# Fused two-block kernel: an opening stage with a hand-written matmul order, grouped modulation sums, and the gate half of convolution group 1 in the two tap banks

## The chip, the cores and the metric

The kernel runs on one core of a Trainium2 chip. Its engines are TensorE (PE; PEld is its weight load), VectorE (DVE), ScalarE (ACT) and GpSimd (POOL); SyncE (SP) issues the DMAs. The metric is the device time of one execution in microseconds (us): the median of three runs.

## The reference, cut to what matters

Two blocks on a sequence of 512 tokens and width 1024, batch 1, all in float32: a first block with two layers (mLSTM and convolution mixer, then an MLP), and a second block (convolution and neighbourhood attention). The change touches the start of layer 0 of the first block:

```python
mod = c_act @ w_ada[l] + b_ada[l]          # c_act = silu(c); 1024 -> 6 x 1024
sh_mix, sc_mix, gt_mix, sh_mlp, sc_mlp, gt_mlp = split(mod, 6)
h = rms_norm(x, g_pre_mix[l]) * (1 + sc_mix) + sh_mix
u = h @ w_in[l]                            # 1024 -> 4096
x_m, z, glu_a, glu_b = split(u, 4)
...
a = glu_a * sigmoid(glu_b)
a = causal_depthwise_conv(a, w_dw, b_dw)   # 31 taps per channel
a = silu(group_layer_norm(a, 8, g_cn, b_cn))
return concat([h_m, a], -1) @ w_out[l]
```

## The kernel before, in words

Activations lie feature-major: 8 tiles `hT[f]` of 128 features by 512 tokens. Every float32 product is made of three matmuls on a high and a low part: `mm3` (L164 to L166) multiplies `wh` with `h` high, `wh` with `h` low, and `wl` with `h` high. A weight unit is loaded by SP into one of 3 buffers `wr`, cast by ACT to `wh` (L155, L1314), and the rest `wl = wr - wh` is made by DVE or POOL (`sub`, L143); `wh` and `wl` have 4 buffers each.

PSUM has three pools: 4 banks `mm` for products, 2 banks `tr` for transposes and small sums, 2 banks `cv` for the long convolution.

**Opening.** `proj_start` makes columns 2048 to 2303 (the value half of convolution group 0) and 3072 to 3327 (its gate half) of layer 0's `w_in` in 4 `mm` banks, in 4 steps `p` of 2 features tiles each: 24 matmuls a step. Before a step, `stage(p)` must have made its two `hT` tiles: `ada_first` adds up 256 shift and 256 scale columns of `w_ada` in 8 matmuls of 32 columns (L439; four of them share the array at four column positions) as each 256 KB load lands, ACT copies the sums (L444), PE transposes them (L447), DVE finishes `mf` (L449, L450, L391); PE transposes the normalised `xn` (L218), ACT scales and shifts it (`hx`, L224), and DVE writes the high and low halves of `h` (L231, L143). For `p == 0`, `x` is loaded and normalised too (L195 to L205).

**Convolution.** There are 4 groups of 256 channels. `glu_cons(g)` makes the gated input `glu` of a group on ACT (L601) and DVE (L602). `taps(g)` puts the group's last tap with the bias into the two `cv` banks on ACT (L584), adds 30 taps to each bank on DVE (L589, 60 instructions a group) and copies both banks to `cacc` on ACT (L593). The `cv` banks serve one group at a time, so group g+1 begins when ACT has copied group g out. `conv_norm` (transposes L696, copies L697, statistics L700 and L701, scaling L711), `conv_gate` (L719, L721, L723, L724) and `conv_split` (L730, `cg`) follow for each group, and the out projection reads `cg`. Between the convolution groups PE makes the rest of `w_in` (`xproj(h)`, with `xm_cons` on ACT and DVE: L628 to L643; `qkv(h)`, whose results ACT copies at L662 and whose transposed `v` it copies at L675; `zproj`).

**What sets the order.** SP issues in program order (`manual_schedule` on SP). On PE, DVE, ACT and POOL a scheduler sets the order when the program is built, by priority, and each engine then runs its queue strictly in that order. `taps` has a much lower priority than all else (`with low(LOWP)`), its ACT instructions as well.

Of the kernel before, what the change touches and what calls it, by code (L numbers as in the profile page):

```python
# [46 lines left out]
def fused_blocks_kernel(ctx: ExitStack, tc: tile.TileContext, I, out):  # L47
# [210 lines left out]
    def proj_start(stage, hT, consumer):  # L258

        ps = [mm() for _ in range(4)]  # L260
        cur = stage(0)
        for p in range(4):
            if p < 3:
                nxt = stage(p + 1)
            h, lo = cur
            for i in range(4):
                for k in range(2):
                    kt, w = 2 * p + k, 2 * (i // 2) + k
                    c = slice((i % 2) * 128, (i % 2) * 128 + 128)
# [158 lines left out]
    def ada_first(p):  # L428


        ps = long_bank()
        wv = wada[0][:, :, 0:2048].rearrange("p k (g n) -> p k g n", g=2)[:, :, :, p * 256:p * 256 + 256]
        for kt in range(0, 8, 2):
            raw = A([128, 2, 2, 256], F32, "wr")
            for k in range(2):
                SP.dma_start(raw[:, k], wv[:, kt + k])
            for k in range(2):
                g = (kt + k) % 4
                PE.matmul(ps[32 * g:32 * g + 32, :], crep[:, kt + k], raw[:, k].rearrange("p g n -> p (g n)"),  # L439
                          start=kt < 4, stop=kt >= 4, tile_position=(0, 32 * g))  # L440
            free(raw)
            yield
# [129 lines left out]
    def mixer(l, pre, units, nxt, pre_next):  # L572
# [34 lines left out]
        if l == 0:  # L607
            proj_start(units, hT, glu_cons(0))
        else:
            proj_first(units, hT, lambda: pre.turn(1), glu_cons(0))  # L610
        for g in range(1, 4):
            projA(wi, [2048 + 256 * g, 3072 + 256 * g], hT, glu_cons(g), eng=None if l == 0 and g == 2 else P)
        free(glu[0])

        if l == 0:
            load_const()
            free(crep)
        q, k, vf, v1, tz, xmh, xch = {}, {}, {}, {}, {}, {}, {}
        wg = A([128, 4, 6, 32], F32, "wg")
        SP.dma_start(wg, I["wg"][l])  # L620

        def xm_cons(h):
# [22 lines left out]
            return fn  # L645

# [648 lines left out]
    def stage(p):  # L1295

        lead = ada_first(p)
        if p == 0:
            for t in range(2):
                next(lead)  # L1300
                load_x(t)
                mix[0].post(t)
        for _ in lead:
            pass
        if p == 0:
            for t in range(2, 4):
                load_x(t)
                mix[0].post(t)
        raw = wrp.tile([128, 4, 256], F32, tag="wr", name="wr")
        for i, c0 in enumerate((2048, 3072)):  # L1310
            SP.dma_start(raw[:, 2 * i:2 * i + 2], wi_[0][:, 2 * p:2 * p + 2, c0:c0 + 256])
        h = whp.tile([128, 4, 256], F32R, tag="wh", name="wh")
        lo = wlp.tile([128, 4, 256], F32R, tag="wl", name="wl")
        S.copy(h, raw)  # L1314
        sub(lo, raw, h, P)
# [116 lines left out]
```

## Time and profile before

| | before |
|---|---|
| median of 3 runs | 2286.89 us (2286.07 to 2290.43) |
| profiled execution, its own time | 2287.21 us |
| its span, first to last instruction | 2285.2 us |
| mean granted TensorE clock | 0.994 |
| PE busy | 2240.0 us (98%) |
| DVE busy | 1530.7 us (67%) |
| ACT busy | 979.1 us (43%) |
| POOL busy | 301.3 us (13%) |

The profile is of one execution. Times in rows are us from the start of the span. A row of the timeline has the start, the length, the engine, the line, the operation, `out<-in` by the program's names, the count, and in brackets the idle time before it with the engine and line that ended it. Ends of matmuls are modelled, so lengths of neighbours overlap; the distance between two starts is the pace. A 32-column sum in float32 shows as two records.

### The profile page before, as it was taken

To read this page: it belongs to the slowest core of one execution; us is meant where nothing else is said; L and a number is where in the kernel's file an instruction comes from. 1 tells how busy PE (TensorE), PEld (TensorE's weight loads), DVE (VectorE), ACT (ScalarE), POOL (GpSimd) and SP (SyncE) were. 2 spreads that over 40 slices of the span, in tenths; PEclk is the share of its full clock that TensorE was granted. 3 is DMA by queue.
4 is the path that set the end of the run, shared out by engine and by line. 5 is a ranking of instruction groups with operands and counts; after the bars stand their busy time and mean duration, and the time that the engine had idled before them with its cause. 6 is when DMAs were issued, how large, how long until landed. Compare 5 with 4: busy or idle time off the path is not lost.

```text
span 2285.2 us, 29859 instructions
## 1 busy us (share of the span) xinstructions
PE 2240.0 (98%) x11164; PEld 1807.5 (79%) x11164; DVE 1530.7 (67%) x3037; ACT 979.1 (43%) x1651; POOL 301.3 (13%) x263
## 2 busy tenths in 40 slices
PE   8999999999999999999999999999999999999998
PEld 3777677878777888767887778888888888878886
DVE  4898998874555678899887643387566574652345
ACT  3557554543323334666543332235545554222232
POOL 1763000000000144400000000000321311000000
PEclk9999999999999999999999999999999999999999
DMA  7632134366565232321436544523211321532331
GB/s 265 211 116 79 55 120 131 128 198 194 179 190 176 87 117 85 92 65 47 148 120 187 177 127 127 170 75 114 88 50 54 98 77 60 172 95 94 99 131 65
DMA packets 194585, 277.69 MB, mean 122 GB/s; under 512 B 13812, under 2 KB 146548, under 8 KB 194440
## 3 DMA queue, kind: packets, MB, share of 16 engines
q1 hardware_dynamic: 194440, 275.78, 37.8%
q8 instruction: 88, 1.44, 0.3%
q14 instruction: 57, 0.47, 0.1%
HBM read 263.68 MB, written 14.37 MB: 122 GB/s over the span
## 4 chain that ended last, share of the span: by engine, by line
PE 74%; DVE 5%; ACT 2%; issue 1%; DMA 0%; POOL 0%; SPq 0%; DVEq 0%; ACTq 0%; POOLq 0%
PE mm L166 22%; PE mm L165 22%; PE mm L164 22%; PE cv L1129 1%; PE tr L1114 1%; PE mm L827 1%; PE mm L851 1%; PE mm L1093 0%; PE mm L1095 0%; DVE h L143 0%; PE tr L218 0%; DVE nt L176 0%; ACT sb L1103 0%; DVE h L231 0%; ACT junk L195 0%
## 5 line engine op out<-in xcount | busy, mean ns | idle before, releaser
L164 PE MATMUL mm<-h,wh 128*128 128x512 f32 (+1 forms) x1728 | 656.8, 381 | 3.8 <-DVE h L231 2.9
L165 PE MATMUL mm<-h,wh 128*128 128x512 f32 (+1 forms) x1728 | 654.3, 379 | 0.7 <-DVE h L143 0.6
L166 PE MATMUL mm<-h,wl 128*128 128x512 f32 (+1 forms) x1728 | 654.4, 379 | 0.1
L155 ACT CAST wh<-wr 128x1024 fp32r<-128x1024 f32 (+1 forms) x318 | 323.3, 1018 | 532.4 <-PE mm L165 249.7
L143 DVE TENSOR_TENSOR wl<-wr,wh 128x1024 fp32r<-128x1024 f32 x254 | 314.0, 1240 | 224.4 <-ACT wh L155 223.4
L164 PEld LDWEIGHTS mm<-h,wh 128*128 128x128 f32 x1728 | 324.7, 188 | 75.2 <-DVE h L231 6.8
L166 PEld LDWEIGHTS mm<-h,wl 128*128 128x128 f32 x1728 | 324.8, 188 | 68.3 <-issue 5.9
L165 PEld LDWEIGHTS mm<-h,wh 128*128 128x128 f32 x1728 | 325.3, 188 | 66.1 <-issue 3.0
L589 DVE SCALAR_TENSOR_TENSOR cv<-glu,vec,cv 128x511 f32<-128x511 f32 (+24 forms) x480 | 327.8, 732 | 7.1 <-ACT cv L584 6.8
L362 DVE SCALAR_TENSOR_TENSOR acc<-wr,csil,acc 128x1024 f32<-128x1024 f32 x91 | 116.1, 1284 | 127.6 <-DMA wr<-in_w_ada_dram 88.4
L165 PE MATMUL mm<-wl,hid 128*128 128x512 f32 x416 | 164.2, 395 | 0.0
L166 PE MATMUL mm<-wh,hid 128*128 128x512 f32 x416 | 164.1, 395 | 0.0
L164 PE MATMUL mm<-wh,hid 128*128 128x512 f32 x416 | 163.4, 395 | 0.0
L143 POOL TENSOR_TENSOR wl<-wr,wh 128x1024 fp32r<-128x1024 f32 (+1 forms) x68 | 137.8, 2033 | 185.0 <-ACT wh L155 144.4
L413 POOL PARTITION_BROADCAST G<-row x5 | 8.3, 1665 | 699.5 <-DVE row L410 383.4
L164 PEld LDWEIGHTS mm<-wh,hid 128*128 128x128 f32 x416 | 78.2, 188 | 19.9 <-issue 0.8
L166 PEld LDWEIGHTS mm<-wh,hid 128*128 128x128 f32 x416 | 78.2, 188 | 18.4
L165 PEld LDWEIGHTS mm<-wl,hid 128*128 128x128 f32 x416 | 78.2, 188 | 18.2
L543 ACT ACTIVATE s<-mm 128x512 f32<-128x512 f32 x64 | 38.0, 594 | 111.3 <-PE mm L166 111.3
L1103 ACT ACTIVATE sb<-sb,nm 128x512 f32<-128x512 f32 x64 | 46.4, 725 | 59.1 <-DVE nm L1101 50.2
L1083 POOL TENSOR_TENSOR bias<-band,amask 128x256 f32<-128x256 f32 x48 | 43.3, 910 | 206.5 <-DVE mx L1098 131.1
L546 DVE CAST hid<-s 128x512 fp32r<-128x512 f32 x64 | 29.0, 457 | 45.9 <-ACT s L544 45.9
(318 smaller groups left out, 3659.4 us busy)
## 6 DMA issues: line engine op xcount, KB each, us to landing
wr<-in_w_in_dram SPq DMA_DIRECT2D x140, 512.0 KB
wr<-in_w_ff_dram SPq DMA_DIRECT2D x128, 512.0 KB
wr<-in_w_ada_dram SPq DMA_DIRECT2D x80, 512.0 KB
wr<-in_w_out_dram SPq DMA_DIRECT2D x32, 512.0 KB
wr<-in_w_mod_dram SPq DMA_DIRECT2D x24, 512.0 KB
wr<-in_w_ada_dram SPq DMA_DIRECT2D x32, 256.0 KB
xd<-x SPq DMA_DIRECT2D x16, 512.0 KB
x<-xd SPq DMA_DIRECT2D x16, 512.0 KB
```

Of the source, the lines that this page charges most:

```text
L143: (eng or V).tensor_tensor(dst, x_, h.bitcast(F32), op=ALU.subtract)
L155: S.copy(h, raw)
L164: PE.matmul(ps, ah, bh, start=first, stop=False)
L165: PE.matmul(ps, ah, bl, start=False, stop=False)
L166: PE.matmul(ps, al, bh, start=False, stop=last)
L362: V.scalar_tensor_tensor(acc, raw, cv[:, kt:kt + 1], acc, op0=ALU.mult, op1=ALU.add)
L543: act(s, ps[m], AF.Relu)
L546: V.tensor_copy(o[:, 0], s)
L589: V.scalar_tensor_tensor(pa[m][:, s:], at[:, m, :512 - s], vv("wdw", l * 248 + (2 * g + m) * 31 + j, 1), pa[m][:, s:], op0=ALU.mult, op1=A ...
L827: PE.matmul(ps[:, :n], k[h][:, kt, j * 128:j * 128 + 128], q[h][:, kt, j * 128:], start=kt == 0, stop=kt == 1)
L1083: P.tensor_tensor(btile[:, b].rearrange("p (c r) -> p c r", r=8), bands[i][:, hh, :, o:o + 32].rearrange("p r c -> p c r"), amask[:, var, ...
L1103: act(sb, sb, AF.Exp, bias=nm, accum_out=sm)
```

## The change

1. The opening takes 6 banks in place of 4: besides the 4 `mm` banks both `cv` banks, which collect columns 3328 to 3583, the gate half of convolution group 1. A step has 36 matmuls in place of 24. Its weights come as two units (4 x 256 and 2 x 256 columns), so a step takes two of the `wr`, `wh` and `wl` buffers.
2. `th_cons` applies the tanh to the two `cv` banks as soon as the opening ends; group 1's own projection then makes its value half only.
3. PE's order in the opening is written by hand (`manual_schedule` on PE): the 8 sums of step p+1 in one piece behind the third of six column groups, their transposes behind the fourth, the transposes of `xn` behind the fifth.
4. The sums go to a `tr` bank, not to a `cv` bank, and wait for all their loads (`ada_load` issues them, `ada_sums` adds them up).
5. For step 0 the 4 loads of `x` are issued ahead of all loads of `w_ada`.
6. In step 0, PE makes 24 transposes of the identity into a spare `tr` bank ahead of the first product.

Moved lines with the same text are left out of the diff.

```diff
-    def proj_start(stage, hT, consumer):
-
-        ps = [mm() for _ in range(4)]
...
+    def proj_start(lead, hT, consumers):
+
+
+        ps = [mm() for _ in range(4)] + [long_bank() for _ in range(2)]
+        with tc.manual_schedule(engines={mybir.EngineType.PE}):
+            cur = lead(0)
+            for _ in range(4):
+                w = next(cur)
+            for p in range(4):
+                nxt = lead(p + 1) if p < 3 else None
+                if nxt:
+                    next(nxt)
+                for i in range(6):
+                    h, lo = w[i // 4]
+                    for k in range(2):
+                        kt, q = 2 * p + k, 2 * ((i % 4) // 2) + k
+                        c = slice((i % 2) * 128, (i % 2) * 128 + 128)
+                        mm3(ps[i], h[:, q, c], lo[:, q, c], hT[kt][:, 0], hT[kt][:, 1], kt == 0, kt == 7)
+                    if nxt and i in (2, 3, 4):
+                        w_next = next(nxt)
+                if nxt:
+                    w = w_next
+        for k, f in enumerate(consumers):
+            f(ps[4 * k:4 * k + 4])
...
+    def ada_sums(raws):
+
+
+        ps = tr()
+        for kt in range(8):
+            g = kt % 4
+            PE.matmul(ps[32 * g:32 * g + 32, :], crep[:, kt], raws[kt // 2][:, kt % 2].rearrange("p g n -> p (g n)"),
+                      start=kt < 4, stop=kt >= 4, tile_position=(0, 32 * g))
+        free(*raws)
...
+        def th_cons(ps):
+
+            ths[1] = [t2([128, 512], F32, "th") for _ in range(2)]
+            for m in range(2):
+                act(ths[1][m], ps[m], AF.Tanh, scale=0.5)
...
+        if l == 0:
+            proj_start(units, hT, (glu_cons(0), th_cons))
...
+            projA(wi, [2048 + 256 * g] + ([] if g in ths else [3072 + 256 * g]), hT, glu_cons(g),
...
         if p == 0:
...
+            load_x(0, 1, 2, 3)
+        raws = ada_load(p)
+        w = []
+        for cols in ((2048, 3072), (3328,)):
...
+        yield
+        rows = ada_sums(raws)
+        yield
+        ada_cols(p, rows)
...
+        if p == 0:
+            bank = tr()
+            for _ in range(24):
+                PE.transpose(bank[:, 0:128], ident, ident)
```

How the instructions stand now, at three places.

PE, from the program's start, before. L439 are the sums (`cv<-wr,crep`), L447 their transposes, L218 the transposes of `xn`:

```order
L439 MATMUL cv<-wr,crep 32x512 x8
L447 MATMUL tr<-ident,rows 128x128 x4
L218 MATMUL tr<-ident,xn 128x128 x5
L439 MATMUL cv<-wr,crep 32x512 x4
L218 MATMUL tr<-ident,xn 128x128 x3
L439 MATMUL cv<-wr,crep 32x512 x2
L164 MATMUL mm<-h_119,wh 128x512 x2
L165 MATMUL mm<-h_119,wh 128x512
L166 MATMUL mm<-h_119,wl 128x512
L439 MATMUL cv<-wr,crep 32x512
```

PE, the same place, now. L453 are the sums, L463 their transposes, L1356 the 24 transposes of the identity:

```order
L453 MATMUL tr<-wr,crep 32x512 x8
L463 MATMUL tr<-ident,rows 128x128 x4
L218 MATMUL tr<-ident,xn 128x128 x8
L1356 MATMUL tr<-ident 128x128 x24
L164 MATMUL mm<-h_119,wh 128x512
L165 MATMUL mm<-h_119,wh 128x512
L166 MATMUL mm<-h_119,wl 128x512
```

The sums of the next step no longer stand between the transposes and the products of step 0; the 24 transposes do.

ACT, where convolution group 1 leaves the `cv` banks and group 2 enters them, before. L593 copies the banks out, L584 starts the next group (`glu_1020` is group 2's gated input); the two copies of `k` here are those of head 1, of four:

```order
L593 COPY cacc<-cv 128x512
L662 COPY k<-mm 128x512
L639 ACTIVATE th<-cv 128x512
L155 CAST wh<-wr 128x512
L662 COPY k<-mm 128x512
L642 CAST xch<-cv 128x512
L675 COPY v_1767<-tr 128x2x256 x2
L593 COPY cacc<-cv 128x512
L697 COPY cacc<-tr 128x512 x2
L584 ACTIVATE cv<-glu_1020,vec 128x512 x2
```

ACT, the same handover, now. L609 copies the banks out, L600 starts group 2 (`glu_1052`); the copies of `q` and `k` (L690) here are those of head 3, the last:

```order
L690 COPY q<-mm 128x512
L155 CAST wh<-wr 128x1024
L690 COPY q<-mm 128x512
L155 CAST wh<-wr 128x1024
L690 COPY k<-mm 128x512
L609 COPY cacc<-cv 128x512 x2
L690 COPY k<-mm 128x512
L703 COPY v_2142<-tr 128x2x256 x2
L155 CAST wh<-wr 128x1024 x2
L600 ACTIVATE cv<-glu_1052,vec 128x512 x2
```

The handover stood among the copies of head 1 and stands among those of head 3: two heads later in ACT's queue.

DVE, the first taps of group 2, before. L589 are taps; L701 to L185 belong to the normalisation of group 0:

```order
L589 SCALAR_TENSOR_TENSOR cv<-glu_1020,vec,cv 128x511
L701 BN_AGGR mv<-bs 128x2
L589 SCALAR_TENSOR_TENSOR cv<-glu_1020,vec,cv 128x511
L703 TENSOR_SCALAR vr<-mv 128x8
L589 SCALAR_TENSOR_TENSOR cv<-glu_1020,vec,cv 128x510
L183 TENSOR_SCALAR ny<-vr 128x8
L589 SCALAR_TENSOR_TENSOR cv<-glu_1020,vec,cv 128x510
L185 TENSOR_TENSOR nt<-ny 128x8
```

DVE, the last taps of group 1 (`glu_842`) and the first of group 2 (`glu_1052`), now. L605 are taps, L649 and L653 are `xproj(3)`'s work, L752 is `conv_gate(0)`'s, L143 are weight remainders for `zproj`:

```order
L605 SCALAR_TENSOR_TENSOR cv<-glu_842,vec,cv 128x482
L649 SCALAR_TENSOR_TENSOR cv<-mm,vec,cv 128x510
L649 SCALAR_TENSOR_TENSOR cv<-mm,vec,cv 128x509
L653 SCALAR_TENSOR_TENSOR cv<-th,cv 128x512
L752 SCALAR_TENSOR_TENSOR cacc<-th,cacc 128x512 x2
L143 TENSOR_TENSOR wl<-wr,wh 128x1024 x4
L605 SCALAR_TENSOR_TENSOR cv<-glu_1052,vec,cv 128x511 x2
L605 SCALAR_TENSOR_TENSOR cv<-glu_1052,vec,cv 128x510 x2
```

The whole normalisation of group 0, the rest of `xproj(3)`, the gating of group 0 and four weight remainders stand ahead of group 2's first tap now. Up to group 3's first tap DVE's queue holds the same instructions as before, in another order, and from the middle of layer 0's out projection on the queues of PE and DVE are in the same order as before.

## Rows read from the trace of the kernel before

**Rows 1.** Page, part 1: busy time, share of the span and instructions of each engine.

```profile
PE 2240.0 (98%) x11164; PEld 1807.5 (79%) x11164; DVE 1530.7 (67%) x3037; ACT 979.1 (43%) x1651; POOL 301.3 (13%) x263
```

**Rows 2.** View of waits, engine PE, whole span: who waited for whom, us in total, times, longest us.

```profile
PE mm L164 <- ACT v L662: 5.0, 2, 2.8
...
PE tr L696 <- ACT v L675: 3.1, 2, 1.6
...
PE mm L164 <- ACT cg L730: 2.1, 1, 2.1
```

**Rows 3.** View of windows, the four stretches from the first tap of group 0 to the end of group 3 (handovers of the `cv` banks at about 121, 192 and 270 us): first the length, then busy time and instructions of PE, PEld, DVE, ACT and POOL in this order, then granted clock, DMA share, GB/s.

```profile
69.18:121.00 51.82, 51.82 (x225) 41.99 (x224) 48.62 (x68) 24.22 (x26) 40.60 (x18) 1.00 0.63 213
121.00:192.00 71.00, 69.43 (x317) 55.17 (x315) 64.72 (x96) 41.90 (x68) 44.27 (x28) 1.00 0.32 96
192.00:270.00 78.00, 75.13 (x359) 54.99 (x358) 72.73 (x162) 50.17 (x94) 9.24 (x12) 0.98 0.27 81
270.00:368.00 98.00, 98.00 (x432) 77.00 (x431) 92.91 (x243) 49.42 (x106) 4.14 (x12) 1.00 0.37 119
```

**Rows 4.** Timeline of ACT and of PE at the end of the convolution: the copies of group 3 out of the `cv` banks, the transposes that wait for them, and the first product with `cg` of group 3.

```profile
367.27 1.21 ACT L593 COPY cacc<-cv 128x512 f32<-128x512 f32 x2 [8.54 <-DVE cv L589]
...
369.28 0.60 PE L696 MATMUL tr<-ident,cacc 128*128 128x128 f32 x4
...
389.85 0.79 PE L164 MATMUL mm<-wha,cg 128*128 128x512 f32 x1 [2.11 <-ACT cg L730]
```

**Rows 5.** Timeline of PE in the opening: the first product; 4 sums (8 records); transposes of sums, then of `xn`, then the next product; two products 30 matmuls apart.

```profile
26.68 1.22 PE L164 MATMUL mm<-h,wh 128*128 128x512 f32 x2
...
37.66 1.06 PE L439 MATMUL cv<-wr,crep 128*32 128x512 f32 x8
...
45.39 0.60 PE L447 MATMUL tr<-ident,rows 128*128 128x128 f32 x4
45.82 1.09 PE L218 MATMUL tr<-ident,xn 128*128 128x128 f32 x8
46.67 0.47 PE L164 MATMUL mm<-h,wh 128*128 128x512 f32 x1
...
64.69 0.39 PE L164 MATMUL mm<-h,wh 128*128 128x512 f32 x1
...
71.66 0.39 PE L164 MATMUL mm<-h,wh 128*128 128x512 f32 x1
```

**Rows 6.** Timelines of ACT, DVE and POOL in the opening: copy of the sums and end of their transposes in step 0; in step 1 a remainder on POOL, `mf` on DVE beside it, and the four `hx` behind it.

```profile
14.02 0.58 ACT L444 COPY rows<-cv 128x512 f32<-128x512 f32 x1 [2.56 <-PE cv L439]
...
15.41 0.17 DVE L449 TENSOR_REDUCE mf<-tr 128x4 f32<-128x16 f32 x1 [1.37 <-PE tr L447]
...
33.95 2.39 POOL L143 TENSOR_TENSOR wl<-wr,wh 128x1024 fp32r<-128x1024 f32 x1 [13.05 <-ACT wh L1314]
...
34.06 2.30 DVE L450 TENSOR_TENSOR mf<-mf,vec 128x4 f32<-128x4 f32 x1
...
36.67 1.93 ACT L224 ACTIVATE hx<-tr,mf 128x256 f32<-128x256 f32 x4 [2.80 <-DVE mf L391]
```

**Rows 7.** View of windows, stretches of the opening, columns as in Rows 3 (the number ahead of the DMA share is the granted clock, 1.00 for 2.4 GHz, 0.50 for 1.2 GHz).

```profile
10.00:20.00 10.00, 6.21 (x26) 2.01 (x25) 7.72 (x31) 6.23 (x16) 1.47 (x1) 0.99 1.08 382
...
15.80:18.80 3.00, 0.01 (x1) 0.00 (x0) 2.63 (x14) 3.00 (x8) 0.27 (x1) 1.00 1.10 367
...
19.90:24.00 4.10, 1.81 (x6) 0.08 (x3) 3.90 (x14) 0.00 (x0) 1.00 (x1) 0.50 1.09 369
...
26.70:30.10 3.40, 3.40 (x8) 1.33 (x6) 0.31 (x1) 0.00 (x0) 0.00 (x0) 0.51 1.10 349
```

**Rows 8.** Timelines of ACT and DVE at the end of the opening: the tanh of the last of its four banks, the first taps of group 0, and the first two weight remainders on DVE behind them.

```profile
67.89 0.58 ACT L601 ACTIVATE th<-mm 128x512 f32<-128x512 f32 x1
...
69.18 7.04 DVE L589 SCALAR_TENSOR_TENSOR cv<-glu,vec,cv 128x511 f32<-128x511 f32 x10
76.93 3.27 DVE L143 TENSOR_TENSOR wl<-wr,wh 128x1024 fp32r<-128x1024 f32 x1 [0.71 <-ACT wh L155]
...
81.42 2.12 DVE L143 TENSOR_TENSOR wl<-wr,wh 128x1024 fp32r<-128x1024 f32 x1
```

**Rows 9.** Timelines of ACT and DVE: the first copy of group 1 out of the `cv` banks, the start of group 2 on ACT, its first tap on DVE; then, on ACT, the first copy of `k` of head 3 and the weight cast behind that head's copies.

```profile
186.47 0.61 ACT L593 COPY cacc<-cv 128x512 f32<-128x512 f32 x1
...
192.80 1.53 ACT L584 ACTIVATE cv<-glu,vec 128x512 f32<-128x512 f32 x2
...
194.54 0.73 DVE L589 SCALAR_TENSOR_TENSOR cv<-glu,vec,cv 128x511 f32<-128x511 f32 x1
...
224.21 0.59 ACT L662 COPY k<-mm 128x512 f32<-128x512 f32 x1 [0.20 <-PE mm L166]
...
227.07 1.08 ACT L155 CAST wh<-wr 128x1024 fp32r<-128x1024 f32 x1
```

**Rows 10.** View of lines, engine DVE, 69.18 to 368 us: busy time and mean ns of one, idle before and its releasers.

```profile
L143 DVE TENSOR_TENSOR wl<-wr,wh 128x1024 fp32r<-128x1024 f32 x22 | 30.3, 1378 | 4.5 <-ACT wh L155 4.5
L636 DVE SCALAR_TENSOR_TENSOR cv<-mm,vec,cv 128x511 f32<-128x511 f32 (+2 forms) x24 | 17.9, 745 | 0.2 <-ACT cv L633 0.2
L640 DVE SCALAR_TENSOR_TENSOR cv<-th,cv 128x512 f32<-128x512 f32 x8 | 9.1, 1135 | 0.6 <-ACT th L639 0.6
...
L143 DVE TENSOR_TENSOR xmh<-mm,xmh 128x512 fp32r<-128x512 f32 x8 | 5.5, 690 | 0.7 <-ACT xmh L628 0.7
```

More of the change, by code (lines that the diff above doesn't have):

```diff
@@ L436, in ada_first, with ada_cols @@
                 SP.dma_start(raw[:, k], wv[:, kt + k])
[L437 to L442, printed above, removed]
+            raws.append(raw)
+        return raws
+    def ada_sums(raws):
[5 more added lines that the diff above has]
+        free(*raws)
         rows = t2([128, 512], F32, "rows")
         S.copy(rows, ps)
+        return rows
+    def ada_cols(p, rows):
         ps = tr()
@@ L605, in glu_cons @@
             return f
[L607 to L617, printed above, removed]
         q, k, vf, v1, tz, xmh, xch = {}, {}, {}, {}, {}, {}, {}
-        wg = A([128, 4, 6, 32], F32, "wg")
-        SP.dma_start(wg, I["wg"][l])
         def xm_cons(h):
@@ L645, in xm_cons @@
             return fn
+        if l == 0:
+            proj_start(units, hT, (glu_cons(0), th_cons))
+        else:
+            proj_first(units, hT, lambda: pre.turn(1), glu_cons(0))
+        for g in range(1, 4):
+            projA(wi, [2048 + 256 * g] + ([] if g in ths else [3072 + 256 * g]), hT, glu_cons(g),
+                  eng=None if l == 0 and g == 2 else P)
+        free(glu[0])
+        if l == 0:
+            load_const()
+            free(crep)
+        wg = A([128, 4, 6, 32], F32, "wg")
+        SP.dma_start(wg, I["wg"][l])
         def xproj(h):
@@ L1295, in stage @@
     def stage(p):
-        lead = ada_first(p)
         if p == 0:
-            for t in range(2):
-                next(lead)
-                load_x(t)
-                mix[0].post(t)
[L1303 to L1315, printed above, removed]
+            load_x(0, 1, 2, 3)
+        raws = ada_load(p)
+        w = []
+        for cols in ((2048, 3072), (3328,)):
+            raw = wrp.tile([128, 2 * len(cols), 256], F32, tag="wr", name="wr")
+            for i, c0 in enumerate(cols):
+                SP.dma_start(raw[:, 2 * i:2 * i + 2], wi_[0][:, 2 * p:2 * p + 2, c0:c0 + 256])
+            w.append(raw)
+        if p == 1:
+            SP.dma_start(vec[:, NLEAD:], I["vec"][:, NLEAD:])
+        if p == 0:
+            for t in range(4):
+                mix[0].post(t)
+        yield
+        rows = ada_sums(raws)
+        yield
+        ada_cols(p, rows)
+        for u, raw in enumerate(w):
+            n = raw.shape[1]
+            h = whp.tile([128, n, 256], F32R, tag="wh", name="wh")
+            lo = wlp.tile([128, n, 256], F32R, tag="wl", name="wl")
+            S.copy(h, raw)
+            sub(lo, raw, h, P)
+            w[u] = h, lo
+        yield
         for half in range(2):
             mix[0].turn(half, (p,))
+        if p == 0:
+            bank = tr()
+            for _ in range(24):
+                PE.transpose(bank[:, 0:128], ident, ident)
         if p == 1:
-            SP.dma_start(vec[:, NLEAD:], I["vec"][:, NLEAD:])
             for nm in ("wcm", "bcm", "gmh", "wdw", "gcn", "bcn", "wc2", "bc2"):
                 V.tensor_scalar(vv(nm), vv(nm), 0.5, None, op0=ALU.mult)
-        return h, lo
+        yield w
     mix[0].hT = [HL(512, f"h{f}") for f in range(8)]
```

24 lines of the change are left out of this document (8 added, 16 removed).

## The prediction

> **What bounds the kernel now.** I read the page's share of busy time first. PE is busy 98% of the span, DVE 67% [rows 1], and PE's list of waits names few, 5.0 us in all for its largest pair [rows 2]. So PE is the bound, but the change touches 26 to 368 us only, and there the windows are to be read. DVE (fourth busy column) fills 48.62 of 51.82, 64.72 of 71, 72.73 of 78 and 92.91 of 98 us [rows 3]: it idles 3.2, 6.3, 5.3 and 5.1 us, 19.9 in 299. What fills it are the taps, in an unbroken chain of four groups through two banks. The reader is to see next that the two bounds meet: ACT copies group 3 out at 367.27, so the first copy is done at about 367.9, and PE comes to its transpose at 369.28 without waiting [rows 4]. The chain has 1.4 us of slack there. Later PE does wait 2.11 us for `cg` of that group [rows 4]. These instructions stand in PE's in-order queue. So a chain later than 1.4 us is paid one for one, and a gain of PE is worth only what the chain gains too.
>
> **Part A, the opening on PE.** Two products 30 matmuls apart start at 64.69 and 71.66: 0.232 us each [rows 5]. A step is 36 x 0.232 = 8.35, plus 8 sums at 1.06 for four, 2.0 in a row, plus 0.43 from the first transpose of sums to the first of `xn`, plus 0.85 from there to the next product [rows 5]: 11.65 us. Three such and the last without a lead make 43.3.
>
> The first product stood at 26.68 [rows 5]. For the new one I go from the copy of the sums of step 0, at 14.02 [rows 6]. The loads of `x`, put ahead, push the last `w_ada` load of the step back by 1 MB at 382 GB/s [rows 7]: 2.7 us, so 16.7. Their transposes were read 1.4 later (15.41 against 14.02), so 18.1. There POOL is to make a remainder, and in step 1 a tiny `mf` step beside such a remainder took 2.30 us (34.06, beside 33.95 for 2.39) [rows 6]. `mf` is then ready at 20.7 and the first two of four `hx` (1.93 us for four) at 21.7. The 24 transposes of the identity cost 0.85/8 each, 2.6 us, at the full clock, twice that at half. PE has nothing to do for some 3 us before, and at 15.8 to 18.8 it had nothing to do either; the granted clock of the next stretch was 0.50 [rows 7]. I take half, 5.2 us: first product at 26.9. Without the blocked `mf` it would be 22.7, with another stall 28.
>
> At the step boundaries PE can wait for `hx` as before, because the sums stand in one piece and the chain copy, transpose, `mf`, `hx` lies behind two or three column groups of 1.4 us. I put 3 us for all three boundaries, bounds 0 (all hidden) and 6 (a blocked `mf` of 2.30 each, less a little). The opening ends on PE at 26.9 + 43.3 + 3 = 73.2, say 73.5, between 66 and 76. Before, the last of four banks was read at 67.89 [rows 8], so PE was done at 67.6. It is 5.9 us later, with 48 more matmuls done, 11.1 us that vanish from group 1's projection: **PE leads by 5.2 us** (2.5 to 10).
>
> **Part B, the start of the chain.** The first tap stood at 69.18, 1.3 behind the last tanh [rows 8]. Now two more tanh, a cast and the start of the banks stand ahead of it on ACT, and two remainders on DVE: 3.5 behind the opening, 77, which is 7.8 later. Those two remainders cost 3.27 and 2.12 us inside the chain before [rows 8] and lie ahead of it now: 7.8 - 5.4 = 2.4 us net.
>
> **Part C, the handover from group 1 to group 2, on which the sign hangs.** Before, ACT began to copy group 1 out at 186.47, started group 2 at 192.80, and its first tap ran at 194.54 [rows 9]. The order of now puts these ACT instructions between the copies of `k` of head 3, and the start behind two casts more. ACT's queue is strict: the two copies wait for a `k` product that PE makes late, and DVE, with its taps of group 1 done, waits behind them. The first `k` copy of head 3 was at 224.21, the cast behind that head at 227.07 [rows 9]. Both come earlier by PE's lead and by one wait for `v` that I take to vanish, 1.6 [rows 2]: 6.8 us. So the cast is at 220.3, two casts of 1.08 [rows 9] follow, and one start of a bank, 1.53/2 [rows 9]; the two copies (1.21 for both [rows 4]) fit partly into ACT's gaps. First tap of group 2: about 223.5, 29 us later than before.
>
> Part of that time DVE has work, since the order moves other work ahead of the tap. By the means of the view of lines [rows 10]: 4 remainders of 1.378, 6 steps of 0.745, 2 of 1.135, 2 `xmh` of 0.69, two gatings of the same shape as those, and some 13 tiny steps of about 0.1 (estimate from the 0.17 of [rows 6]), less one tap of 0.73 [rows 9]: 15 us. The chain is 29 - 15 = 14 us behind. With B's 2.4, DVE idles about 29 - 15 - 2.4 = 11.6 us before that tap.
>
> Of this a part comes back. The last two stretches held 5.3 + 5.1 = 10.4 us of idle DVE [rows 3], idle because inputs were late; with PE ahead and DVE behind, inputs are there. I take 5 of it, bounds 1 and 10.4. Then 14 - 5 = 9, less the slack of 1.4: **PE is 7.6 us late at group 3's transposes.** Behind them PE's order is as before, so this lateness goes to the end; bounds below zero come from the opening (case 2 and 3).
>
> The rest is costed at nothing: grouped sums have the same count of matmuls; two units a step move the same bytes, and ACT's two casts lie beside products (ACT is under 60% busy in the stretches of [rows 3]); if that cover is gone, a cast of 1.08 a step, inside the 6 us bound of A.
>
> The sum: 2287.2 (the profiled execution) + 7.6 = 2294.8; against the median, 0.3 below that execution, 2294.5. I forecast **2295**.
>
> **A rule against the trace.** The stretch at half clock behind an idle PE is the row: 0.50 at 19.9 to 24.0, 0.51 still at 26.7 to 30.1, with 8 matmuls in 3.4 us [rows 7]. No row has transposes alone ahead of products. The Trainium skill, page "TensorE: Matmul & The Clock Gate", section "Part 4: PE-mode transpose", says that the full clock does not engage for transpose-mode work, since it does not count as PE-busy in the same way. No run here shows that yet. By that rule the 24 transposes would buy nothing; it is case 4 below, which is priced from rows.
>
> **The rivals.**
> 1. *Main case.* As summed: 2291.5 to 2300.
> 2. *Faster: the lead passes through.* If the boundaries cost nothing and the first product is at 22.7, PE leads by 10; the first `k` copy is then at about 212.5, the first tap of group 2 at 218.7, 24 later, and if all 10.4 us of idle come back the chain is 24 - 15 - 10.4 - 1.4 below zero, -2.8, and no later than that on PE: 2284; a handover at still less cost (first tap by 213) gives PE's own lead of 5 to 8: 2279 to 2282. For it: PE is 98% busy, so its lead is real time. Against it: ACT's queue, which is a strict order. The point: group 2's first tap must come before 194.5 + 15 + 5 + 1.4 = 216 for any gain.
> 3. *Same.* Either only the idle time comes back (14 - 10.4 - 1.4 = 2.2: 2289) or only the opening is early (first tap 218.7, 24 - 15 - 5 - 1.4 = 2.6: 2289.5).
> 4. *Slower still: the transposes do not bring the clock.* They cost 5.2 us and the first 8 products run as in 26.7 to 30.1, 3.4 us for what takes 1.9 at full clock. With another stall in step 0 the lead falls to some 2 us, the first tap comes at 226.7, the sum is 32 - 15 - 5 - 1.4 = 10.8: 2298. With 1 us of idle time saved, 2302. For it: the clock's rows [rows 7]; against it: PE is at least not idle during them.
> 5. *It does not do what it says.* The order shows six banks filled in the opening and the grouped sums; I give this nothing.
>
> **How the numbers follow.** What a measurement of this kernel can tell from no change is about 0.2%, 4.6 us: faster is under 2282.3, slower over 2291.5. Chances: case 1 0.45, case 4 0.2, case 3 and the upper half of case 2 (2282.3 to 2291.5) 0.2, the lower part of case 2 0.15. So faster 0.15, same 0.2, slower 0.65. The range reaches from the start of case 2's lower part, 2281, to case 4's upper end, 2302, and leaves out about 0.1 on either side. The slower cases alone span 2291.5 to 2302.
>
> **What would show it.** In the changed profile: A, the first product near 27 with 0.5 of the clock ahead of it, the last of six banks read at about 73.5; if that is under 69, the lead is 10. B, the first tap near 77. C, the decisive row: the two copies of group 1 on ACT after 217, the first tap of group 2 at about 223, and an idle time of some 12 us on DVE released by ACT's start of the bank. At the end of the convolution, ACT's copy of group 3 near 376 and an idle PE ahead of its transposes or of the product with `cg`. The prediction is wrong if DVE does not idle at that handover, or if the copies of group 1 come when its taps end; and the mechanism is wrong if DVE idles there and PE still comes to the out projection early.

## The result and the profile after

The changed kernel takes 2311.86 us (median of 4 runs, 2309.47 to 2314.24), the kernel before 2287.86 in the runs beside it: a ratio of 1.0101, 95% interval 1.0089 to 1.0113. It is 24 us slower where 7.6 were forecast, and outside the range given.

Page of the changed kernel, part 1, as [rows 1]:

```profile
PE 2237.9 (97%) x11188; PEld 1811.9 (78%) x11188; DVE 1531.3 (66%) x3037; ACT 979.6 (42%) x1653; POOL 300.5 (13%) x265
```

The work is the same but for the 24 transposes; what is new is waiting, and more half clock (mean granted clock 0.990, 0.994 before). View of waits of PE, whole span, as [rows 2]:

```profile
PE tr L724 <- ACT cacc L609: 13.7, 2, 13.4
PE mm L164 <- DVE h L231: 10.1, 5, 7.4
...
PE mm L164 <- DVE cv L649: 4.9, 2, 3.4
```

The largest wait is on the convolution chain: PE stands idle until ACT has copied group 2 out. Timeline of PE at that place:

```profile
291.17 1.11 PE L724 MATMUL tr<-ident,cacc 128*128 128x128 f32 x4 [13.45 <-ACT cacc L609]
```

In the kernel before PE did not wait at group 2's transposes:

```profile
270.30 0.60 PE L696 MATMUL tr<-ident,cacc 128*128 128x128 f32 x4
```

View of windows of the changed kernel, the four stretches of the chain from its first tap to group 3's copy, columns as in [rows 3]:

```profile
83.04:133.60 50.56, 50.56 (x220) 40.90 (x219) 44.92 (x67) 19.32 (x20) 31.36 (x15) 1.00 0.53 181
133.60:228.55 94.95, 89.49 (x395) 69.62 (x394) 77.23 (x136) 60.53 (x104) 47.57 (x32) 0.96 0.26 79
228.55:290.50 61.95, 49.12 (x244) 33.57 (x242) 57.98 (x121) 29.01 (x55) 2.22 (x4) 0.93 0.24 75
290.50:389.86 99.36, 97.31 (x411) 77.05 (x412) 92.63 (x243) 49.49 (x104) 3.52 (x12) 0.94 0.36 117
```

The reader is to take length less DVE's busy time (the third busy figure behind the length): DVE idles 5.6, 17.7, 4.0 and 6.7 us, 34.1 in all against 19.8 in the same chain before, which is 14 us more, 11.4 of them in the second stretch (17.7 against 6.3). DVE is busy 272.8 us there against 278.3 before. Timelines of ACT and of PE at the end of the chain, as [rows 4]:

```profile
389.86 1.22 ACT L609 COPY cacc<-cv 128x512 f32<-128x512 f32 x2 [8.14 <-DVE cv L605]
...
412.61 0.80 PE L164 MATMUL mm<-wha,cg 128*128 128x512 f32 x1 [2.11 <-ACT cg L758]
```

Timelines of ACT and of DVE at the end of group 1, as [rows 9]:

```profile
228.07 0.66 ACT L690 COPY k<-mm 128x512 f32<-128x512 f32 x1
228.55 1.15 ACT L609 COPY cacc<-cv 128x512 f32<-128x512 f32 x2
...
233.30 1.06 ACT L155 CAST wh<-wr 128x1024 fp32r<-128x1024 f32 x1 [1.19 <-DMA wr<-in_w_in_dram]
234.26 1.48 ACT L600 ACTIVATE cv<-glu,vec 128x512 f32<-128x512 f32 x2
```

```profile
213.94 0.71 DVE L605 SCALAR_TENSOR_TENSOR cv<-glu,vec,cv 128x482 f32<-128x482 f32 x1
...
217.50 0.88 DVE L653 SCALAR_TENSOR_TENSOR cv<-th,cv 128x512 f32<-128x512 f32 x1 [1.42 <-ACT th L652]
223.40 1.29 DVE L752 SCALAR_TENSOR_TENSOR cacc<-th,cacc 128x512 f32<-128x512 f32 x2 [5.02 <-ACT th L751]
226.84 1.23 DVE L143 TENSOR_TENSOR wl<-wr,wh 128x1024 fp32r<-128x1024 f32 x1 [2.14 <-ACT wh L155]
228.27 1.23 DVE L143 TENSOR_TENSOR wl<-wr,wh 128x1024 fp32r<-128x1024 f32 x1 [0.21 <-ACT wh L155]
232.14 1.23 DVE L143 TENSOR_TENSOR wl<-wr,wh 128x1024 fp32r<-128x1024 f32 x1 [2.64 <-ACT wh L155]
234.39 1.23 DVE L143 TENSOR_TENSOR wl<-wr,wh 128x1024 fp32r<-128x1024 f32 x1 [1.02 <-ACT wh L155]
235.53 2.72 DVE L605 SCALAR_TENSOR_TENSOR cv<-glu,vec,cv 128x511 f32<-128x511 f32 x4
```

Group 1's last tap is done at 214.6; ACT copies it out 14 us later, behind head 3's `k`, and the next tap follows at 235.5. In between DVE waits six times, 12.45 us. None of these waits is ended by ACT's start of the bank (L600): four end on casts of `wh`, two on a tanh, all on ACT, and the tap itself follows the last remainder without a wait. ACT (the figure behind DVE's) is busy 19.71 of 20.90 us there; view of windows:

```profile
214.60:235.50 20.90, 19.44 (x96) 15.59 (x95) 8.40 (x10) 19.71 (x36) 5.32 (x6) 1.00 0.37 110
```

The chain also starts late. Timelines of PE, DVE and POOL at the opening's last step, and of PE at its end:

```profile
68.49 0.79 PE L164 MATMUL mm<-h,wh 128*128 128x512 f32 x1 [7.44 <-DVE h L231]
...
79.45 0.40 PE L166 MATMUL cv<-h,wl 128*128 128x512 f32 x1
```

```profile
61.28 2.46 DVE L143 TENSOR_TENSOR h<-hx,h 128x256 fp32r<-128x256 f32 x1
63.67 4.77 DVE L231 CAST h<-hx 128x256 fp32r<-128x256 f32 x2
...
69.03 0.28 DVE L231 CAST h<-hx 128x256 fp32r<-128x256 f32 x1
69.34 0.43 DVE L143 TENSOR_TENSOR h<-hx,h 128x256 fp32r<-128x256 f32 x1
```

```profile
61.05 4.89 POOL L143 TENSOR_TENSOR wl<-wr,wh 128x1024 fp32r<-128x1024 f32 x2
65.90 2.38 POOL L367 TENSOR_TENSOR acc<-acc,wr 128x1024 f32<-128x1024 f32 x1
```

Beside POOL's remainders and its gemv addition (L367), two casts of `h` take about 2.4 us each, where one takes 0.28 when POOL is done, and a subtraction 2.46, where one takes 0.43. The Trainium skill, page "SBUF — State Buffer", section "SBUF: two separate sides", describes an exclusive lock of a port pair that VectorE and GpSimd share, held for a whole instruction, for VectorE instructions with two SBUF inputs or in a 2-port mode. The trace agrees: these steps take as long as POOL's instructions beside them (2.38 to 2.45 us each). PE waits 7.44 us and then runs at half clock; view of windows, columns as above:

```profile
68.49:74.00 5.51, 5.51 (x12) 4.09 (x13) 1.24 (x4) 1.07 (x1) 2.38 (x1) 0.50 0.37 139
```

### The profile page after: what moved, and what is told of

It reads as the page before. It is cut to its first block, busy times and chain, and to the rows that moved or that the text cites. A ratio compares the mean times of both kernels' runs of the same rounds, so it can differ in the third digit from the quotient of the medians.

```text
span 2309.7 us, 29922 instructions
## 1 busy us (share of the span) xinstructions
PE 2237.9 (97%) x11188; PEld 1811.9 (78%) x11188; DVE 1531.3 (66%) x3037; ACT 979.6 (42%) x1653; POOL 300.5 (13%) x265
## 4 chain that ended last, share of the span: by engine, by line
PE 78%; DVE 7%; ACT 2%; issue 1%; DMA 0%; POOL 0%; SPq 0%; DVEq 0%; ACTq 0%; POOLq 0%
PE mm L164 23%; PE mm L166 23%; PE mm L165 23%; PE mm L879 2%; DVE cv L605 1%; PE mm L855 1%; PE cv L1157 1%; PE tr L1142 1%; ACT sb L1131 0%; DVE h L143 0%; PE tr L218 0%; DVE sb L1126 0%; DMA wr<-in_w_in_dram 0%; PE mm L1121 0%; PE mm L1123 0%
## 5 line engine op out<-in xcount | busy, mean ns | idle before, releaser
L164 PE MATMUL mm<-h,wh 128*128 128x512 f32 (+1 forms) x1712 | 651.6, 381 | 11.3 <-DVE h L231 10.1
L166 PE MATMUL mm<-h,wl 128*128 128x512 f32 (+1 forms) x1712 | 647.4, 379 | 0.1
L143 DVE TENSOR_TENSOR wl<-wr,wh 128x1024 fp32r<-128x1024 f32 x254 | 313.0, 1236 | 232.9 <-ACT wh L155 231.8
L605 DVE SCALAR_TENSOR_TENSOR cv<-glu,vec,cv 128x511 f32<-128x511 f32 (+18 forms) x480 | 326.3, 731 | 8.2 <-ACT cv L600 8.0
L143 POOL TENSOR_TENSOR wl<-wr,wh 128x1024 fp32r<-128x1024 f32 (+1 forms) x70 | 138.2, 1982 | 165.2 <-ACT wh L155 136.0
L165 PEld LDWEIGHTS mm<-wl,hid 128*128 128x128 f32 x416 | 78.1, 188 | 18.1
```

The lines of the kernel that those rows point to most:

```text
L143: (eng or V).tensor_tensor(dst, x_, h.bitcast(F32), op=ALU.subtract)
L164: PE.matmul(ps, ah, bh, start=first, stop=False)
L165: PE.matmul(ps, ah, bl, start=False, stop=False)
L166: PE.matmul(ps, al, bh, start=False, stop=last)
L605: V.scalar_tensor_tensor(pa[m][:, s:], at[:, m, :512 - s], vv("wdw", l * 248 + (2 * g + m) * 31 + j, 1), pa[m][:, s:], op0=ALU.mult, op1=A ...
```

## The experiments

All kernels compute the reference in full. In the diffs `low(...)` is the priority of what it holds, `step()` issues the next load of the gemv `ada_pair` and the work on it. Line numbers of the edited kernels lie up to 8 above those of the changed one. The table holds all runs; the ratio is to the kernel before as run beside each; "idle" is DVE's from its first tap to ACT's copy of group 3, length less busy time in the view of windows; "cg" is PE's first product with group 3's `cg`. Times are medians, the other columns are of the profiled execution. In runs 8, 10 and 11 PE came to the product with `cg` without a wait; in all other rows it waited for `cg`, and the product follows the copy by 22.5 to 23.1 us.

| | us | ratio to before, interval | first tap | idle | copy | cg |
|---|---|---|---|---|---|---|
| before | 2287.9 | | 69.2 | 19.8 | 367.3 | 389.9 |
| changed | 2311.9 | 1.0089 to 1.0113 | 83.0 | 34.1 | 389.9 | 412.6 |
| 1 handover | 2301.0 | 1.0040 to 1.0066 | 80.2 | 23.7 | 377.4 | 400.1 |
| 2 POOL free | 2312.2 | 1.0084 to 1.0112 | 75.5 | 36.1 | 387.0 | 409.6 |
| 3 both | 2302.0 | 1.0045 to 1.0070 | 72.1 | 29.5 | 377.0 | 399.9 |
| 4 no transposes | 2311.6 | 1.0085 to 1.0116 | 84.8 | 31.6 | 389.1 | 411.9 |
| 5 four banks | 2294.0 | 1.0010 to 1.0028 | 76.2 | 23.5 | 373.9 | 396.9 |
| 6 four, POOL free | 2298.6 | 1.0028 to 1.0053 | 71.9 | 27.5 | 375.4 | 398.0 |
| 7 before, handover | 2288.1 | 0.9989 to 1.0006 | 69.8 | 18.1 | 365.4 | 387.9 |
| 8 both, `glu` low | 2303.7 | 1.0052 to 1.0080 | 72.1 | 30.5 | 376.5 | 407.7 |
| 9 handover, two steps | 2296.3 | 1.0024 to 1.0049 | 81.9 | 19.8 | 374.3 | 397.0 |
| 10 handover, gemv later | 2312.6 | 1.0093 to 1.0120 | 76.1 | 31.6 | 390.8 | 417.9 |
| 11 before, both of 10 | 2310.0 | 1.0083 to 1.0110 | 76.9 | 32.5 | 387.1 | 416.0 |
| 12 two steps | 2307.4 | 1.0070 to 1.0097 | 85.9 | 30.0 | 385.9 | 408.8 |
| 13 six, mended | 2294.6 | 1.0016 to 1.0039 | 83.4 | 17.1 | 373.1 | 395.8 |
| 14 four, mended | 2288.1 | 0.9991 to 1.0009 | 71.5 | 18.0 | 365.2 | 387.8 |
| 15 six, free | 2293.4 | 1.0008 to 1.0026 | 73.7 | 22.1 | 369.6 | 392.6 |
| 16 six, free, other gap | 2295.9 | 1.0022 to 1.0045 | 73.7 | 27.5 | 375.0 | 398.1 |

**Run 1, the handover.** Theory 1 of the prediction against the opening as rival.

```diff
-            with low(LOWP):
-                pa = [long_bank() for _ in range(2)]
+            pa = [long_bank() for _ in range(2)]
+            with low(LOWP if l else 0):
                 ... act(pa[m], ...)
+            with low(LOWP):
                 ... taps
+            with low(LOWP if l else 0):
                 for m in range(2):
                     S.copy(acc[:, m], pa[m])
```

> Edit: in layer 0 only, ACT's instructions that start and copy out a convolution group get the normal priority; the taps on DVE keep the low one. The opening is that of the changed kernel. In ACT's queue the copies of group 1 then stand behind 13 copies of q, k and v instead of 23. Theory 1 (the place of this handover in ACT's queue costs the time, the late opening only adds to it): first tap of group 2 at about 203 to 207 instead of 235.5, no wait of PE at the transposes of group 2, 2288 to 2294 us. Theory 2 (the late end of the opening, 11 us with its stall of 7.4 and its half clock, is what is paid, and the handover is late because of it): first tap of group 2 earlier but PE later elsewhere, 2300 to 2310 us.

Timeline of ACT in run 1, the same handover (L611 copies out):

```profile
211.46 0.56 ACT L611 COPY cacc<-cv 128x512 f32<-128x512 f32 x1
...
212.32 0.57 ACT L611 COPY cacc<-cv 128x512 f32<-128x512 f32 x1
212.78 1.49 ACT L600 ACTIVATE cv<-glu,vec 128x512 f32<-128x512 f32 x2
```

The copies now follow the taps, the wait of PE at group 2 is gone, DVE's idle time falls by 10.4 us and the time by 10.8. That is less than half of the 24 us. Theory 1 missed: the first tap of group 2 came at 213.6 and not by 207, and 2301.0 lies above its 2294. The time falls into the range of theory 2, at its lower end, and PE waits elsewhere, as that theory has it: 5.2 us for `v` and 3.5 at the first `q`. Runs 2 and 3 put theory 2 to the test.

**Runs 2 and 3, the stall of the opening.** Here and below `wait(n)` is a generator that lets n steps pass.

```diff
-            pending.append(ada_pair(l, 3, "gpl", True))
+            pending += [wait(4), ada_pair(l, 3, "gpl", True)]
-                  eng=None if l == 0 and g == 2 else P)
+                  eng=None if l == 0 and g in (1, 2) else P)
```

> Edit: POOL is kept free at the end of the opening: the first steps of the gemv on ACT and POOL start four weight units later, and the two weight remainders of group 1's value half are made by DVE. ACT's handover of groups 1 to 2 stays behind 24 copies of q, k and v. Theory 1: the stall of 7.4 us before the last step and its half clock go, the opening ends near 71 instead of 79.6, the handover is still bound to head 3, first tap of group 2 near 227, 2302 to 2306 us. Theory 2: 2286 to 2294 us.

> Both edits, of the handover's priority and of POOL's work. Theory 1: no wait of PE at group 2's transposes, PE's lead of 5 to 8 us shows as far as the chain lets it, 2281 to 2287 us. Theory 2: as with the edit of POOL alone, within 3 us.

Timelines of PE and of ACT in run 2 (L168 is the product, L369 the gemv on ACT):

```profile
63.54 0.49 PE L168 MATMUL mm<-h,wh 128*128 128x512 f32 x1 [0.37 <-DVE h L235]
...
162.46 0.76 PE L168 MATMUL mm<-xch,wh 128*128 128x512 f32 x1 [8.91 <-DVE cv L653]
```

```profile
151.32 1.15 ACT L369 ACTIVATE wr<-wr,csil 128x1024 f32<-128x1024 f32 x1 [3.26 <-DMA wr<-in_w_ada_dram]
...
152.88 0.58 ACT L645 CAST xmh<-mm 128x512 fp32r<-128x512 f32 x1
...
155.76 0.61 ACT L656 ACTIVATE th<-cv 128x512 f32<-128x512 f32 x1
```

With POOL idle the stall of 7.44 is 0.37 and the first tap 7.6 us earlier: POOL was its cause. But the time did not move in either run (2312.2 against 2311.9, 2302.0 against run 1's 2301.0), and both theories missed. The gemv that I pushed back stood among `xproj`'s work now: ACT waits for loads of `w_ada` with the casts of `xmh` and the tanh behind it, DVE waits for them, and PE waits 8.91 us for the first `q`. That made a fourth theory, on the gemv (runs 9 to 12).

**Run 4, the 24 transposes left out.**

> Edit: the 24 transposes of the identity ahead of the first product are left out. If they keep the clock up (theory of the change): the first products run at 1.2 GHz for some 3 us as in the kernel before, first product at about 21.5 to 22 instead of 24.0, but end of step 0 about the same, time within 2 us of the changed kernel, 2310 to 2314. If the clock does not fall without them either: end of step 0 some 2.5 us earlier, 2308 to 2311. If products at half clock last for more than one step: later, 2314 to 2320.

Views of windows, the changed kernel, then run 4, then run 12:

```profile
21.40:24.20 2.80, 2.80 (x25) 2.80 (x26) 2.29 (x8) 0.84 (x2) 0.00 (x0) 1.00 1.10 376
24.20:28.00 3.80, 3.80 (x19) 3.05 (x17) 1.34 (x1) 1.57 (x2) 1.76 (x1) 1.00 1.08 374
```

```profile
21.40:24.20 2.80, 0.82 (x2) 0.44 (x2) 2.35 (x7) 1.75 (x4) 0.91 (x1) 0.53 1.09 368
24.20:28.00 3.80, 3.80 (x9) 2.99 (x10) 1.29 (x2) 1.56 (x2) 1.32 (x1) 0.50 1.08 381
```

```profile
21.40:24.20 2.80, 2.75 (x16) 2.76 (x17) 2.35 (x8) 0.91 (x2) 0.07 (x1) 0.65 1.09 379
24.20:28.00 3.80, 3.80 (x20) 3.42 (x19) 1.58 (x1) 1.57 (x2) 2.00 (x1) 0.81 1.08 371
```

With the transposes the granted clock stayed at 1.00 behind an idle time of 2.9 us; without them PE idled 4.0 us, the clock was half (0.53, 0.50), and 9 records ran in the second stretch in place of 19. That the transposes keep the clock does not follow from this: in run 12 PE idled 2.9 us as well, and it fell all the same. Of the 14 profiles with the transposes, all behind 2.9 us of idle time, the 24 took 2.84 us in 6 (the changed kernel and runs 1, 3, 5, 8 and 9) and 4.2 to 4.5 in the other 8. But in run 12 the clock also rose, from 0.65 to 0.81 over the two stretches, with nothing but transposes on PE up to the first product at 25.71, and that product and those behind it ran at the full pace (0.32 us to the second start, then 0.23), as in all 14. So transposes do bring the clock here, against the section of the Trainium skill that the prediction weighed (page "TensorE: Matmul & The Clock Gate", "Part 4: PE-mode transpose"). In time they are worth nothing that can be measured: 2311.6 against 2311.9. Without them the first product stands 0.6 us earlier (23.38), step 0 ends 1.9 us later (its next sums at 30.15 and not 28.27) and the first tap comes 1.8 us later, but the copy of group 3 comes 0.8 us earlier.

**Runs 5 and 6, four banks.** `ps` has 4 banks, `cols` one unit, `th_cons` goes; run 6 adds the edit of run 2.

> Edit: the opening takes only the four banks, as in the kernel before; the gate half of group 1 goes back to its own projection. The hand-written order, the grouped sums, the early loads of x and the 24 transposes stay. Theory 3 (the end of the convolution chain on DVE is its start plus its busy time plus its idle time; the 48 products of the gate half stand ahead of the chain's start, and PE's time saved by them later is time in which DVE is the bound): opening over at 57 to 63 instead of 79.6, first tap at 59 to 66, PE's first product with cg at 385 to 392, 2281 to 2288 us. Rival (the hand-written order with its sums in one piece loses the time, whatever the banks): 2295 us or more.

> Four banks, and POOL kept free at the end of the opening as in the second run. Theory 3: a stall at the last step, if four banks alone have one, goes; first tap 0 to 6 us earlier than with four banks alone, and the time by at most as much: 2279 to 2288 us. Rival: as four banks alone, 2295 or more.

Run 5 is 18 us better than six banks, but no match for the kernel before: its opening has stalls at all three step boundaries (1.5; 1.5; 3.5, 1.2 and 1.8) and the first tap is 7 us late. Its time lies between the two forecasts. Run 6 removes the last two of these stalls and is 4.6 us slower than run 5; PE waits 5.5 us at the first `q` there, as in run 2 behind the displaced gemv. Its time is the rival's, but run 14 below clears the hand-written order.

**Run 7, a control.** The edit of run 1 in the kernel before.

> Kernel before, with the normal priority for ACT's handovers in layer 0 and nothing else. In it the handovers stood close to the end of the taps already. Theories 1 and 3: no change, 2285 to 2291 us; so what this edit gave in the changed kernel belongs to the change. If the edit is worth something by itself: 2283 or less.

No change: what run 1 gained belongs to the change.

**Run 8** adds `low(LOWP)` around the gated inputs of groups 2 and 3 on DVE to run 3.

> As the third run (both edits), and the gated inputs of groups 2 and 3 on DVE get the low priority of the taps, so that DVE does not wait for their products in the middle of group 0's taps (two waits of 5.5 us there). Theory 3: idle time of DVE in the chain falls from 29.5 to 20 to 23, PE's first product with cg at 392 to 394 instead of 400, 2292 to 2296 us. Rival (PE, not DVE, sets the end there, and a wait only moves): 2299 to 2303 us.

The wait moved and did not go: PE then waits 6.2 us for the tanh and 8.5 for the convolution of `xproj`, and comes to the product with `cg` at 407.7 without waiting for it. The forecast missed; the rival was right in kind, its range short by 0.7 us.

**Runs 9 to 12, the gemv.** Run 9 is run 1 with two steps behind the opening, run 12 has these steps alone; run 10 is run 1 with `wait(18)`, run 11 the same in the kernel before.

```diff
             proj_start(units, hT, (glu_cons(0), th_cons))
+            step()
+            step()
```

> As the first run (normal priority of the handover), and two steps of the gemv's loads are issued right behind the opening, because the change took two weight units away that carried one step each. In the changed kernel ACT waits 4.74 us for such a load at 147, right ahead of the first cast of xmh (147.9), in the kernel before the last such wait is at 132 and the cast at 140. Theory 4 (part of the lost time is ACT waiting in its queue for loads of w_ada ahead of xproj's first work, which then makes DVE and PE wait at the first q): last such wait before 142, wait of PE for the first q under 1 us, 2295 to 2299 us. Against it: 2300 to 2303, as the first run.

> As the first run, and the gemv starts 18 weight units later, so that none of it stands ahead of the first xmh in ACT's queue and POOL makes only two remainders at the end of the opening. Theory 4: wait of PE at the first q gone, stall at the last step of the opening 4 to 5 us, first tap at 76 to 78, 2289 to 2297 us; if the waits only move behind xmh, 2298 to 2303.

> Control: the kernel before with both of these edits. Theory 4: in it the gemv was done before xproj began, so there is nothing to gain: 2285 to 2291 us, or slower if its waits now stand among xproj's work. Under 2283 would say that the gemv cost the kernel before too.

> Changed kernel with two steps of the gemv's loads right behind the opening and nothing else. In the order of ACT that comes out, the copies of group 1 stand behind 12 copies of q, k and v, not 23, though their priority is untouched. Theory 1 (their place costs about 11 us): 2296 to 2301 us, as with the normal priority. If the priority itself and not the place did it: 2308 or more.

Timelines of ACT, the last wait for `w_ada` ahead of the first cast of `xmh`: the kernel before, the changed one, run 9:

```profile
131.53 1.15 ACT L356 ACTIVATE wr<-wr,csil 128x1024 f32<-128x1024 f32 x1 [3.82 <-DMA wr<-in_w_ada_dram]
...
140.14 0.59 ACT L628 CAST xmh<-mm 128x512 fp32r<-128x512 f32 x1 [4.22 <-PE mm L166]
```

```profile
146.82 1.15 ACT L365 ACTIVATE wr<-wr,csil 128x1024 f32<-128x1024 f32 x1 [4.74 <-DMA wr<-in_w_ada_dram]
147.88 0.56 ACT L641 CAST xmh<-mm 128x512 fp32r<-128x512 f32 x1
```

```profile
131.25 1.15 ACT L365 ACTIVATE wr<-wr,csil 128x1024 f32<-128x1024 f32 x1 [3.77 <-DMA wr<-in_w_ada_dram]
...
141.82 0.59 ACT L643 CAST xmh<-mm 128x512 fp32r<-128x512 f32 x1 [4.17 <-PE mm L166]
```

The change took two weight units out of the projections, each of which carried one step of the gemv; its last load came later, into the path of `xmh`. Two steps earlier give 4.7 us with the handover mended (run 9 against 1) and 4.5 without (run 12 against the changed kernel), and the handover gives 10.8 and 11.1: the two add up. PE's wait for the first `q` is gone in both, as run 9's forecast had it. Run 12 missed both of its ranges (2296 to 2301, and 2308 or more). In it one bank of group 1 is copied at 205.46, the other only at 229.37, behind head 3, so its handover is still late. PE waits 11.8 us at group 2's transposes there. Runs 10 and 11 missed: a gemv that stands among `xproj` and `qkv` costs 22 us in the kernel before as well. So it gained nothing to start it that late.

**Runs 13 to 16, all mended, six banks and four.** They join the edit of run 1, DVE for group 1's remainders, and a gemv that starts after the opening and is made up for by extra steps ahead of groups 2 and 3: `wait(2)` and 2 + 2 steps (13), `wait(2)` and 1 + 1 with four banks (14), `wait(4)` and 6 (15) or 4 (16) ahead of group 3.

> Six banks, normal priority of the handover; the gemv starts two weight units later, so that POOL makes none of it in the opening, and makes up for it with two extra steps ahead of each of groups 2 and 3, so that all of it still stands ahead of the first xmh; DVE makes the two remainders of group 1's value half. If the late start is what is left: opening over near 71, first tap 72 to 74, 2287 to 2291 us. If the 48 products ahead of the chain and the lost slack are: 2293 to 2298.

> The same with four banks (one extra step ahead of each of groups 2 and 3). If the 48 products ahead of the chain cost something beyond the stall: opening over near 67, first tap 71, and 2 to 5 us less than with six banks, 2284 to 2290. If not: the same time as with six banks, within 2 us.

> As run 13, with the gemv four weight units later and six extra steps ahead of group 3. If the late start is what is left: no stall at the last step above 1 us, opening over near 71, first tap 72 to 76, PE's first product with cg at 387 to 391, 2286 to 2290 us. If the slack lost with the gate half is: first tap as said, but idle time of DVE in the chain 26 us or more, and 2292 to 2298 us.

> The same with four extra steps ahead of group 3. The same two cases; where the six extra loads in one piece delay group 3's weights, this one is 1 to 4 us faster, otherwise within 2 us.

Run 14 is the kernel before again, to 0.1%: the hand-written order, the grouped sums, the early `x` and the transposes, taken together and beside the other edits of this set, neither give nor cost. Run 13 kept the stall (3.4, 1.2 and 1.8 us) and is 6.5 us slower; its time is that of its second case, but the early first tap that it was to test did not come (83.4). Run 15 has no stall (0.36) and a first tap within 4.5 us of the kernel before, and is still 5 us slower than run 14. Both of its cases missed in part: the time is the second one's, the idle time (22.1, not 26 or more) is not. Run 16 was to be as fast as run 15 or faster; its median is 2.5 us higher, but its executions spread from 2291.8 to 2301.4 and the intervals overlap, so neither is shown to be better. View of waits of DVE in the chain, run 15, then run 14 (L635 is the gated input):

```profile
DVE glu L635 <- ACT th L634: 13.4, 2, 7.4
```

```profile
DVE glu L635 <- ACT th L634: 4.8, 3, 2.9
```

With the gate half done early, DVE waits longer for the tanh of groups 2 and 3 (6.0 and 7.4 us in run 15) with taps queued behind. In the chain's sum run 15 copies group 3 out 4.4 us later than run 14: the first tap is 2.2 later, idle time 4.1 more, busy time 1.8 less. PE has waits of its own there that run 14 lacks, 5.6 us for `v` and 5.0 for the tanh. That the tanh is what makes the 5 us is argued from these rows, not shown: no run took its wait away alone (run 8 moved it).

## Why the prediction was wrong in size

- **The chain is tied to PE and its lateness is paid one for one: right.** Copy of group 3 +22.6 us, product with `cg` +22.8, end of the profiled span +24.5.
- **Part A failed.** "I put 3 us for all three boundaries" was mis-sized: they cost 12.2 (79.5 - 23.97 - 43.3). The last step alone cost 7.44 us of waiting and some 2.7 us of half clock (12 records in 5.51 us). The row for it was there: a DVE step beside a POOL remainder at 2.3 us in [rows 6]. I used it in step 0, where it came as summed, in these rows of DVE and POOL:

```profile
17.99 2.19 DVE L400 SCALAR_TENSOR_TENSOR mf<-mf,vec 128x2 f32<-128x2 f32 x1
...
17.81 3.59 POOL L143 TENSOR_TENSOR wl<-wr,wh 128x1024 fp32r<-128x1024 f32 x2 [8.22 <-ACT wh L1347]
```

  But I capped it at the boundaries, where three POOL instructions in a row met three DVE ones. The first product came at 23.97 rather than 26.9, as the clock was full over the transposes; that was luck of this execution, since in 8 of 14 profiles it was not. The opening ended at 79.5 rather than 73.5, and "PE leads by 5.2 us" became a lag of 0.8 (11.9 later, 11.1 of work done).
- **Part B right in form:** start +13.9 rather than +7.8, for that reason; DVE's busy time in the chain fell by 5.6 where 5.4 was summed for the remainders.
- **Part C right in place, late by 12 us.** The handover stood behind head 3 as the order shows; first tap at 235.5 rather than 223.5. PE's missing lead (6.0) and the 3.4 us that it lost at the first `q` to the gemv's loads make 9.4 of the 12; I had not costed these loads at all ("the rest is costed at nothing"). DVE's idle time there is 12.45 us; 11.6 was summed. That they agree is partly luck: the sign that I named, ACT's start of the bank, ends none of these waits, they stand ahead of it in the queues of ACT and DVE. And the list of DVE's other work, summed to 15, adds up to 16.5 from the figures given, which would have made the idle time 10.1 and the forecast 1.5 us less. The lateness did not show as lateness of group 3 alone: PE met it one group earlier, in the 13.45 us wait.
- **"I take 5 of it" failed:** the last two stretches idle 10.7 us, as before (10.4 in [rows 3]). Nothing came back. PE was not ahead there, and the granted clock was 0.93 and 0.94 in these stretches against 0.98 and 1.00 before; what that cost no run tells apart.
- **The slack of 1.4 us failed too:** PE had met the chain at group 2 already, and at group 3 the transposes came 1.9 us behind the start of the copy (391.77) as they had before (2.0). Nothing was left to take up.
- **The sum** 7.8 - 5.4 + 11.6 - 5 - 1.4 = 7.6 measured 13.9 - 5.6 + 14.3 + 0.2 = 22.8 to `cg`: start, busy time, idle time, and from the copy to the product.
- **In time,** by the runs: handover 11 us and gemv's place 4.5, each from two pairs of runs; six banks in place of four 5 or so (runs 13 and 15 against 14). The opening's stall is put at 1 to 3 from runs 13 and 9 against 15, which differ in the gemv's place as well, so that share is argued.
- **The rivals.** Rival 4 was wrong in its cause: the transposes ran at full clock in this profile and brought it in others. In rival 2 two figures do not follow from part A's: without the blocked `mf` the first product stands at 24.6 rather than 22.7, and with 22.7 the lead is 12.7 rather than 10. The 7.6 does not hang on these two.

Open: where the last 1.7 us between `cg` and the end come from. Edited kernels lose up to 5.5 us there (run 2).

No version beat the kernel before; run 14 equals it.

## What to carry to other kernels

When two engines are tied, work moved ahead of the start of the second engine's chain can delay that chain (13.9 us here, 2.2 where the stall was gone, run 15 against 14), and the lead that it gives to the first engine buys nothing until the second catches up. In strict queues look at what else rides on the moved work: here two weight units carried two steps of a gemv, whose loads then stalled ACT ahead of a critical cast. Where a scheduler fixes the order, find each low-priority copy that frees a resource, and see behind whose late input it now stands.

## What the runs showed of the hardware

DVE casts of 128x256 elements took about 2.4 us each beside POOL's 2.4 us instructions and 0.28 alone; a subtraction 2.46 and 0.43. The granted clock behind 2.9 us of idle PE stayed at 1.00 in the changed kernel's profile and fell in another (0.65 in run 12) at the same place of the same program text; over 24 transposes of the identity it rose again, and the products behind them ran at full pace.
